# Modulation tiles issued earlier and attention's steps reordered in a two-layer hybrid transformer kernel

## The chip, the cores and the metric

One core of one Trainium2 chip runs the whole kernel. The metric is the device time of one execution in microseconds, as the median of several runs. Of the engines, PE is TensorE (PEld its weight load), DVE is VectorE, ACT is ScalarE, POOL is GpSimd, and SP (SyncE) issues DMAs.

## The reference, cut to what matters

Two layers over 256 latent tokens and 256 context tokens, width 1024. Each layer is a half-step SwiGLU, a token mixer and a half-step SwiGLU, and each of the three is scaled, shifted and gated by a modulation vector of nine parts:

```python
mod_l = (jax.nn.silu(c) @ w_mod[i] + b_mod[i]).reshape(b, N_MOD, 1, D_MODEL)
mod_c = (jax.nn.silu(c_ctx) @ w_mod[i] + b_mod[i]).reshape(N_MOD, 1, D_MODEL)
x_lat = x_lat + 0.5 * mod_l[:, 2] * swiglu(modulate(x_lat, norm_gain[i, 0], mod_l[:, 0], mod_l[:, 1]), ffn_a_in[i], ffn_a_out[i])
...
def neighbourhood_attention(q, k, v, k_ctx, v_ctx, rpb):
    s = jnp.concatenate([s_win.reshape(b, h, GRID_W, n_win), s_ctx], axis=-1)
    p = jax.nn.softmax(s, axis=-1).astype(v.dtype)
def dense_attention(q, k, v):
    p = jax.nn.softmax(s, axis=-1).astype(v.dtype)
```

The mixer of layer 0 is attention (8 heads) beside a long convolution, that of layer 1 is retention with 4 heads. Both streams, latent and context, pass through it; only the latents come out of the last layer.

## The kernel before, in words

Every matrix product is made of three TensorE products, high by high, low by high, high by low, so each weight tile (128x1024) is split into a high and a low part: ACT copies the high part (`whi`, line 92), DVE subtracts it for the low part (`wlo`, line 186). A call of `w_get` splits three tiles ahead of the one it hands out. The order on each engine is the order of the calls in the program; nothing is reordered. PSUM tiles of the pool `ps` have seven buffers.

The modulation vectors of all but the first two parts are 128 tiles of `w_mod` (128x1024 each), read in a fixed order (layer 0 parts 2 to 8, then layer 1). `mod_step` takes the next one: DVE multiplies the tile by the conditioning row and sums it up (`junk`, line 272), twice, once per stream, or once for parts 5 to 8 of layer 1 (tile 96 onwards); then `m_dma` issues the load of the next tile from POOL's queue (line 257). The two buffers of `wm` mean that this load waits for the reduction of the tile before. Where `mod_step` is called is written out by hand at each place.

The stages in order, with their place in the trace: the first SwiGLU of layer 0 (`ffn`, about 57 to 413 us, 22 pairs of input tiles in three pieces, each piece followed by `out_gemm`); the attention and convolution mixer (`mixer0`, to 668); two SwiGLUs in which most products are made of seven instead of eight half products (`ffn_fast` with class `Fast`, to 1375; its first piece makes pairs 2 and 3 in the plain way, then starts the seven-product pairs with `ramp` and `cycle`); retention (`mixer1`, to 1667); the last SwiGLU on the latents alone (`ffn` with `lat_only`).

In `mixer0` the loop `for i in range(12)` makes one projected tile per step and calls `attend(i)`. For head pair b = i // 2, an even step makes the latents' scores (`scores_lat`), an odd one the context's (`scores_ctx`); each returns a closure for the exponentials (`exps`, ACT) and one for the normalisation (`norm`, DVE). The even step after that transposes both heads' probabilities (`transposes`: per head two latent blocks `ptp`, one context block `ptc`), and the odd one after it multiplies them by the values. The scores' high and low parts of queries and keys come from `qk_split`. `z_conv` makes the short convolution's tile of each step between them.

In `mixer1` each of the 4 heads does `qk_parts` (POOL makes the low parts, line 974), four `tiles` of the values' projection with `mod_step` between them, the split of the values (`vlo`, line 216) which frees the four PSUM buffers `pv`, two `tiles` of the gate, and the next head's `scores` (`pst`).

Of the kernel before, what the change touches and what calls it, by code (L numbers as in the profile page):

```python
# [57 lines left out]
def body(ctx, tc, I, out):  # L58
# [550 lines left out]
    def in_tile(n0=0, n1=TOK, ahead=3):  # L609
        return tile_mm(w_get(ahead), n0, n1)  # L610
# [243 lines left out]
    def ffn_fast(i, l, n, norm_in, norm_out):  # L854
        fast = None
        for h, (jf, jl) in enumerate(PIECES):
            Gt = []
            last = h == len(PIECES) - 1

            def evac(pa, pb):  # L860
                sg = page(name="sg")
                act(sg, pa, AF.Silu)
                V.tensor_tensor(out=sg, in0=sg, in1=pb, op=ALU.mult)
                g = (page(dt=F32R, name="ghi"), page(dt=F32R, name="glo"))
                split_to(sg, g[0], g[1])
                drop(sg)
                Gt.append(g)

            if h == 0:
                p = first_group(norm_in, lambda p: evac(p[0], p[1]))  # L870
                hs = half_sums(norm_in)
                evac(p[2], p[3])
                next(hs)
                for j in range(2, FAST[i]):
                    end = j == FAST[i] - 1
                    wa, wb = w_get(), w_get()
                    pa = tile_mm(wa)
                    next(hs, None)
                    if end:
                        fast = Fast(jl - FAST[i])  # L880
                        fast.ramp()
                    else:
                        w_split()
                    pb = tile_mm(wb)
                    next(hs, None)
                    evac(pa, pb)
                    if not end:
                        mod_step()
                next(hs, None)
            Gt.extend(fast.run())  # L890
            if last:
                h_free()
            if h == 0:
                set_gate(l, n)
            pend_free.extend(Gt)

            def ramp():
                nonlocal fast
                fast = Fast(PIECES[h + 1][1] - PIECES[h + 1][0])
                fast.ramp()  # L900

            out_gemm(Gt, jl - jf, 1, l, n, False, norm_out if last else None,
                     ramp=None if last else ramp, mods=2 if last else KB - 1)
            free_acts()

    def ffn(l, n, norm_in, norm_out, lat_only=False):
        w = L if lat_only else TOK
        for h, (jf, jl) in enumerate(PIECES):
            Gt = []
            last = h == len(PIECES) - 1  # L910

            def evac(pa, pb, shift=None):
                sg = page([P, w], name="sg")
                if shift is None:
                    act(sg, pa[:, :w], AF.Silu)
                    V.tensor_tensor(out=sg, in0=sg, in1=pb[:, :w], op=ALU.mult)  # L916
                else:
                    act(sg, pa[:, :w], AF.Silu, bias=shift[:, 0:1])
                    V.scalar_tensor_tensor(out=sg, in0=pb[:, :w], scalar=shift[:, 1:2], in1=sg,
                                           op0=ALU.add, op1=ALU.mult)  # L920
                g = (page([P, w], F32R, "ghi"), page([P, w], F32R, "glo"))
                split_to(sg, g[0], g[1])
                drop(sg)
                Gt.append(g)

            j0 = 0
            if h == 0:
                if norm_in is None:
                    q, cs = pre.pop("first")
                    w_split()  # L930
                    for t in range(0, 6, 2):
                        if t:
                            w_split()
                        evac(q[t], q[t + 1], cs[:, t:t + 2])
                    w_split()
                    drop(*q)
                elif callable(norm_in):
                    p = norm_in()
                    evac(p[0], p[1])
                    evac(p[2], p[3])  # L940
                else:
                    p = first_group(norm_in, lambda p: evac(p[0], p[1]))
                    evac(p[2], p[3])
                j0 = len(Gt)
            for j in range(jf + j0, jl):
                pa = in_tile(0, w)
                pb = in_tile(0, w)
                evac(pa, pb)
                full = next(FILT["gen"], True)
                if not lat_only or j < 5:  # L950
                    mod_step(1 if lat_only or not full else 2)
            if last:
                h_free()
            if h == 0:
                set_gate(l, n)
            pend_free.extend(Gt)
            out_gemm(Gt, jl - jf, 1, l, n, lat_only, norm_out if last else None, mods=2 if last else KB)
            free_acts()
# [296 lines left out]
    def mixer0(norm_in, norm_out):  # L1255
# [145 lines left out]
            return prc, exps, norm  # L1401

        def transposes(prs, prc):
            pt = [page([P, 2, 256], name="pt") for _ in range(2)]
            for qb in range(2):
                p = ps([P, 4, P], name="ptp")
                for kb in range(4):
                    T.transpose(p[:, kb, :], prs[qb][:, kb * P:(kb + 1) * P], ident)
                for i in range(2):
                    dst = pt[i][:, :, qb * P:(qb + 1) * P]  # L1410
                    if i:
                        V.tensor_copy(dst, p[:, 2 * i:2 * i + 2, :])
                    else:
                        act(dst, p[:, 2 * i:2 * i + 2, :], AF.Copy)
            p = ps([P, 2, 2, P], name="ptc")
            for qb in range(2):
                for kb in range(2):
                    T.transpose(p[:, kb, qb, :], prc[:, qb, kb * P:(kb + 1) * P], ident)
            ptc = page([P, 2, 256], name="ptc")
            act(ptc, p.rearrange("p a b c -> p a (b c)"), AF.Copy)  # L1420
            drop(*prs, prc)
            return pt, ptc

        def values(b, turned):

# [16 lines left out]
        def attend(i):  # L1442

            b, odd = divmod(i, 2)
            if odd and b - 1 in turned:
                values(b - 1, turned.pop(b - 1))
            if not odd and b - 1 in lat:
                prs, prc = lat.pop(b - 1)[0], con.pop(b - 1)[0]
                turned[b - 1] = [transposes(prs[j], prc[j]) for j in range(2)]
            if b < 4 and not odd:  # L1450
                lat[b] = scores_lat(b)
                left.append(lat[b][1:])
            if b < 4 and odd:
                con[b] = scores_ctx(b)
                left.append(con[b][1:])
                for a in qks.pop(b):
                    drop(*a)
                for j in range(2):
                    load_bias(2 * b + 2 + j)


        blkr = one.tile([P, P], F32R, name="blkr")
# [20 lines left out]
        for c in range(2):  # L1483
            w = [w_get(), w_get(2)]
            for tb in range(4):
# [7 lines left out]
                    T.matmul(o, lhsT=H[k][1][:, hs_], rhs=wk[0][:, ws_], start=False, stop=k == KB - 1)  # L1493
                if (c, tb) in ((0, 1), (1, 0)):
                    qk_step()
            mod_step(2)
        for tb in range(4):
            vt.append(page(name="vt"))
            act(vt[tb], pv[tb], AF.Copy)

        qk_split(0)
        load_bias(0)
        load_bias(1)
        dft = []
# [25 lines left out]
        for i in range(12):  # L1530
            p = in_tile()
            attend(i)
            if i < 8:
                ex, nor = left.pop(0)
                c = z_conv(i // 2, p, i % 2 == 0)
                if i % 2 == 0:
                    next(c)
                    ex()
                    next(c, None)
                    held = nor  # L1540
                else:
                    held()
                    ex()
                    next(c)
                    nor()
                    if i < 7:
                        qk_split(i // 2 + 1)
                    next(c, None)
            else:
                x0c.extend(conv(p, i - 8, "x0c"))  # L1550
            if i in (2, 4, 6, 8):
# [60 lines left out]
    def mixer1(norm_in, norm_out):  # L1612
# [33 lines left out]
        for h in range(4):  # L1646
            pa, pb = in_tile(0, L), in_tile(0, L)
            q = page(name="qT")
            rope_to(q[:, :L], q[:, L:], pa[:, :L], pb[:, :L])
            qT.append(q)  # L1650
            if h % 2:
                mod_step()
            if h == 0:
                parted(kT[0], 0)
                parted(kT[0], 1)
            if h == 1:
                parted(qT, 0)
# [106 lines left out]
        for h in range(4):  # L1764
# [2 lines left out]
            pv = [ps(name="pv") for _ in range(4)]  # L1767
            for n in range(4):
                tiles(4, pv, n)
                if n in (1, 2):  # L1770
                    mod_step(2)
                if n == 0 and prev:
                    o_trans(h - 1, prev)
            vh = []
            for tb in range(4):
                vh.append((page(dt=F32R, name="vhi"), page(dt=F32R, name="vlo")))
# [164 lines left out]
```

## Time and profile before

| | |
|---|---|
| median of 3 runs | 1862.87 us (1859.59, 1862.87, 1862.88) |
| profiled execution, its own time | 1861.55 us |
| its span, first to last instruction | 1859.8 us |
| PE busy | 1823.5 us, 98% |
| DVE busy | 1403.1 us, 75% |
| ACT busy | 828.8 us, 45% |
| POOL busy | 195.7 us, 11% |
| DMA | 306 MB, 165 GB/s |
| reductions of modulation tiles (line 272) | 224, 289.1 us of DVE |

Busy times say how long an engine had an instruction in work. In the timeline each row has the start in us from the span's start, the duration of the merged run of instructions, the engine, the line, the operation, what it writes and reads, the shapes, their number, and in brackets how long the engine stood idle before it and what ended that.

### The profile page before, as it was taken

The page shows a single profiled execution, that of the slowest core. Times are in us where ns is not written, and L with a number is a line of the kernel's source. Part 1 is how long each engine was busy: PE and PEld are TensorE (multiplying, and loading weights), DVE is VectorE, ACT ScalarE, POOL GpSimd, SP SyncE. Part 2 cuts the span into 40 slices and gives each one's busy share as a digit, 9 for nine tenths or more (in the row PEclk, how much of TensorE's full clock was granted, in tenths as well). Part 3 has the DMA queues.
Part 4 walks back from the last instruction along what each step waited for, and adds up shares of the span by engine and source line. Part 5 has one row for each costly group of instructions (what it writes and reads, how often), then busy time and mean ns, then how long its engine had stood idle before and what let it go on. Part 6 is the DMA issues. An engine that isn't in the chain of part 4 may idle for free.

```text
span 1859.8 us, 28832 instructions
## 1 busy us (share of the span) xinstructions
PE 1823.5 (98%) x11264; PEld 1606.0 (86%) x11264; DVE 1403.1 (75%) x2303; ACT 828.8 (45%) x1388; POOL 195.7 (11%) x271
## 2 busy tenths in 40 slices
PE   7999999999999999999999999999999899999999
PEld 4788888888777898898998889989999788899999
DVE  6678797777877878888876788778777776687554
ACT  4422222245564356264464653626543354455443
POOL 2020010001102100111110001111001111000000
PEclk9999999999999999999999999999999999999999
DMA  9446565532422334576673356757635444475563
GB/s 358 174 165 216 171 214 184 189 125 80 159 69 91 125 108 125 171 193 195 174 215 114 80 174 180 209 164 198 200 103 175 137 140 155 159 242 171 179 200 105
DMA packets 98074, 306.01 MB, mean 165 GB/s; under 512 B 10897, under 2 KB 11921, under 8 KB 97810
## 3 DMA queue, kind: packets, MB, share of 16 engines
q1 hardware_dynamic: 67986, 216.08, 34.7%
q0 software_dynamic: 29952, 88.09, 17.9%
q8 instruction: 88, 1.44, 0.3%
q14 instruction: 48, 0.39, 0.1%
HBM read 303.08 MB, written 1.05 MB: 164 GB/s over the span
## 4 chain that ended last, share of the span: by engine, by line
PE 56%; DVE 7%; issue 5%; ACT 4%; DMA 1%; POOL 0%; POOLq 0%; ACTq 0%; DVEq 0%
PE pA L709 9%; PE po L245 6%; PE po L244 6%; PE po L243 6%; PE pC L709 5%; PE pi L243 3%; PE pi L245 3%; PE pi L244 3%; PE pB L709 2%; PE fg L244 1%; PE fg L243 1%; PE fg L245 1%; PE pv L1685 1%; PE pv L1683 1%; PE pv L1684 1%
## 5 line engine op out<-in xcount | busy, mean ns | idle before, releaser
L92 ACT ACTIVATE whi<-raw 128x1024 fp32r<-128x1024 f32 (+2 forms) x434 | 422.1, 1000 | 267.6 <-PE po L244 119.3
L186 DVE TENSOR_TENSOR wlo<-raw,whi 128x1024 fp32r<-128x1024 f32 (+1 forms) x286 | 340.8, 1212 | 65.5 <-ACT whi L92 64.0
L243 PE MATMUL pi<-hhi,whi 128*128 128x512 f32 (+1 forms) x912 | 318.8, 350 | 0.2 <-ACT ptc L92 0.2
L245 PE MATMUL pi<-hhi,wlo 128*128 128x512 f32 (+1 forms) x912 | 318.1, 349 | 0.0
L244 PE MATMUL pi<-hlo,whi 128*128 128x512 f32 (+1 forms) x912 | 317.4, 348 | 0.0
L272 DVE CUSTOM_DVE_ANT_0 junk<-wm,scb,cst 128x1024 bf16<-128x1024 f32 x224 | 289.1, 1291 | 30.7 <-DMA wm<-in_wmt_dram 26.4
L243 PE MATMUL po<-ghi,whi 128*128 128x512 f32 (+1 forms) x776 | 269.9, 348 | 0.3 <-ACT ghi L92 0.3
L244 PE MATMUL po<-glo,whi 128*128 128x512 f32 (+1 forms) x776 | 269.5, 347 | 0.1
L245 PE MATMUL po<-ghi,wlo 128*128 128x512 f32 (+1 forms) x776 | 269.6, 347 | 0.0
L243 PEld LDWEIGHTS pi<-hhi,whi 128*128 128x128 f32 x912 | 171.7, 188 | 26.8 <-issue 1.5
L245 PEld LDWEIGHTS pi<-hhi,wlo 128*128 128x128 f32 x912 | 171.5, 188 | 23.7
L244 PEld LDWEIGHTS pi<-hlo,whi 128*128 128x128 f32 x912 | 171.6, 188 | 23.6
L695 DVE TENSOR_TENSOR wlo<-raw,whi 128x1024 fp32r<-128x1024 f32 (+1 forms) x144 | 153.7, 1088 | 43.9 <-ACT whi L92 43.4
L243 PEld LDWEIGHTS po<-ghi,whi 128*128 128x128 f32 x776 | 145.9, 188 | 20.4 <-ACT ghi L92 0.5
L244 PEld LDWEIGHTS po<-glo,whi 128*128 128x128 f32 x776 | 145.9, 188 | 20.4 <-DVE glo L216 0.3
L245 PEld LDWEIGHTS po<-ghi,wlo 128*128 128x128 f32 x776 | 145.9, 188 | 19.9
L257 POOL DMA_DIRECT2D wm<-in_wmt_dram x128 | 71.2, 556 | 857.3 <-DVE mod L272 838.2
L434 DVE SCALAR_TENSOR_TENSOR x<-po,gate,x 128x256 f32<-128x256 f32 x192 | 86.4, 479 | 59.8 <-PE po L245 59.4
L92 ACT ACTIVATE ghi<-sg 128x512 fp32r<-128x512 f32 (+1 forms) x52 | 28.2, 541 | 183.3 <-DVE sg L916 172.3
L709 PE MATMUL pC<-hlo,whi 128*128 128x256 f32 x288 | 81.0, 281 | 0.6 <-DVE hlo L216 0.6
L709 PE MATMUL pC<-hhi,wlo 128*128 128x256 f32 x288 | 81.1, 282 | 0.1
L709 PE MATMUL pC<-hhi,whi 128*128 128x256 f32 x288 | 80.5, 279 | 0.0
(405 smaller groups left out, 3897.6 us busy)
## 6 DMA issues: line engine op xcount, KB each, us to landing
raw<-in_ffi_dram SPq DMA_DIRECT2D x176, 512.0 KB, 4.4
wm<-in_wmt_dram POOLq DMA_DIRECT2D x128, 512.0 KB, 3.9
raw<-in_rt_dram SPq DMA_DIRECT2D x64, 512.0 KB, 4.3
raw<-in_ffo_dram SPq DMA_DIRECT2D x64, 448.0 KB, 4.1
raw<-in_ffi_dram POOLq DMA_DIRECT2D x72, 256.0 KB, 5.7
raw<-in_ffo_dram SPq DMA_DIRECT2D x32, 512.0 KB, 4.5
raw<-in_ev_dram SPq DMA_DIRECT2D x32, 512.0 KB, 4.3
raw<-in_ffi_dram SPq DMA_DIRECT2D x36, 256.0 KB, 3.7
```

The costliest lines, as they stand in the source:

```text
L92: S.activation(out=out, in_=in_, func=func, **k)
L186: V.tensor_tensor(out=lo[:, :n], in0=t[:, :n], in1=f(hi[:, :n]), op=ALU.subtract)
L243: T.matmul(o, lhsT=w[0][:, c0:c1], rhs=x[0][:, x0:x1], start=start, stop=False)
L244: T.matmul(o, lhsT=w[0][:, c0:c1], rhs=x[1][:, x0:x1], start=False, stop=False)
L245: T.matmul(o, lhsT=w[1][:, c0:c1], rhs=x[0][:, x0:x1], start=False, stop=stop)
L257: G.dma_start(out=t, in_=I["wmt"][n])
L272: V.tensor_tensor_reduce(out=junk, in0=t, in1=scb[:, s, :], scale=1.0, scalar=bcol, op0=ALU.mult, op1=ALU.add, accum_out=MOD[l][:, idx, b, ...
L434: V.scalar_tensor_tensor(out=xs(s, m), in0=p[:, c0:c0 + L], scalar=gate[:, m, s:s + 1], in1=xs(s, m), op0=ALU.mult, op1=ALU.add)
L695: V.tensor_tensor(out=w[1][:, :c], in0=src, in1=f(w[0][:, :c]), op=ALU.subtract)
L709: T.matmul(o, lhsT=w[a][:, c0 + j * P:c0 + (j + 1) * P], rhs=x(j)[b][:, x0(j):x0(j) + L], start=first and j + a + b == 0, stop=j == 3 and ...
L1683: T.matmul(po[tb], lhsT=H[k][0][:, hs_], rhs=w[0][:, ws_], start=k == 0, stop=False)
L1684: T.matmul(po[tb], lhsT=H[k][0][:, hs_], rhs=w[1][:, ws_], start=False, stop=False)
```

## The change

In `ffn_fast` the `mod_step` after the last plain pair is dropped. In `ffn` of layer 0 seven pairs (j = 8, 10, 12, 15, 17, 18, 20) get one more, between their two products; the last `ffn` gets one more, at j = 5. In `mixer0` the second `mod_step(2)` of the values' projection becomes one `mod_step` after `qk_split(0)`. In `mixer1` the one at h = 3 of the query projections goes, and the four per head (two after each of tiles 1 and 2) become three (one after each of tiles 0, 1 and 2). The number of tiles in all stays 128.

In attention the latents' normalisation follows its exponentials in the same step instead of standing over to the next one; `qk_split(b + 1)` moves ahead of the exponentials of the odd step; the context's normalisation comes after the convolution's tile is done; and the transposes take both heads' four latent blocks first and then the two context blocks.

```diff
@@ ffn_fast
                     evac(pa, pb)
-                    if not end:
-                        mod_step()
@@ ffn
                 pa = in_tile(0, w)
+                if not lat_only and j in (8, 10, 12, 15, 17, 18, 20):
+                    mod_step()
                 pb = in_tile(0, w)
                 evac(pa, pb)
                 full = next(FILT["gen"], True)
-                if not lat_only or j < 5:
+                if not lat_only or j < 6:
                     mod_step(1 if lat_only or not full else 2)
@@ transposes (prs, prc are now of both heads)
+            pt = [[page([P, 2, 256], name="pt") for _ in range(2)] for _ in range(2)]
+            for j in range(2):
+                for qb in range(2):
+                    p = ps([P, 4, P], name="ptp")
...
+                drop(*prs[j])
+            ptc = []
+            for j in range(2):
+                p = ps([P, 2, 2, P], name="ptc")
...
+                ptc.append(page([P, 2, 256], name="ptc"))
+                act(ptc[j], p.rearrange("p a b c -> p a (b c)"), AF.Copy)
+                drop(prc[j])
+            return list(zip(pt, ptc))
@@ attend
-                turned[b - 1] = [transposes(prs[j], prc[j]) for j in range(2)]
+                turned[b - 1] = transposes(prs, prc)
...
                     load_bias(2 * b + 2 + j)
+                if b < 3:
+                    qk_split(b + 1)
@@ values' projection of mixer0
-            mod_step(2)
+            if c == 0:
+                mod_step(2)
...
         qk_split(0)
+        mod_step()
@@ loop over i of mixer0
-                if i % 2 == 0:
-                    next(c)
-                    ex()
-                    next(c, None)
-                    held = nor
-                else:
-                    held()
-                    ex()
-                    next(c)
-                    nor()
-                    if i < 7:
-                        qk_split(i // 2 + 1)
-                    next(c, None)
+                next(c)
+                ex()
+                next(c, None)
+                nor()
@@ mixer1, query projections and heads
-            if h % 2:
+            if h == 1:
                 mod_step()
...
-                if n in (1, 2):
-                    mod_step(2)
                 if n == 0 and prev:
                     o_trans(h - 1, prev)
+                if n < 3:
+                    mod_step()
```

## Rows read from the trace of the kernel before

**Rows 1.** The page's first part: busy time, share and instructions of each engine.
```profile
PE 1823.5 (98%) x11264; PEld 1606.0 (86%) x11264; DVE 1403.1 (75%) x2303; ACT 828.8 (45%) x1388; POOL 195.7 (11%) x271
```
**Rows 2.** PE's waits by releaser: total us, times, longest us.
```profile
PE pst L243 <- DVE vlo L216: 7.4, 1, 7.4
...
PE psc L1342 <- DVE qklo L216: 0.8, 1, 0.8
...
PE ptp L1408 <- DVE pr L1373: 0.8, 2, 0.6
```
**Rows 3.** Stretches: start:end length, busy us of each engine, granted clock, DMA share, GB/s.
```profile
125.00:400.00 275.00, 275.00 (x1201) 223.21 (x1200) 224.34 (x335) 75.16 (x97) 25.87 (x49) 1.00 0.57 192
...
513.40:516.70 3.30, 3.30 (x14) 2.12 (x11) 3.23 (x10) 0.23 (x1) 0.00 (x0) 0.50 0.00 0
...
1471.20:1478.60 7.40, 0.13 (x2) 0.00 (x0) 5.46 (x10) 0.00 (x0) 1.05 (x2) 0.81 0.58 213
1478.60:1482.60 4.00, 3.90 (x15) 3.71 (x16) 3.57 (x6) 0.39 (x1) 0.00 (x0) 0.50 0.44 135
...
714.00:727.00 13.00, 10.04 (x73) 8.73 (x72) 11.30 (x17) 7.95 (x16) 0.00 (x0) 1.00 0.15 44
```
**Rows 4.** Timeline of DVE, ACT and PE at the first start of seven-product pairs.
```profile
709.26 1.28 DVE L272 CUSTOM_DVE_ANT_0 junk<-wm,scb,cst 128x1024 bf16<-128x1024 f32 x1
...
712.13 0.42 DVE L631 TENSOR_TENSOR sx<-hf 128x256 f32<-128x256 f32 x1
...
708.52 1.69 ACT L92 ACTIVATE hf<-hf,mod 128x256 f32<-128x256 f32 x4
...
722.47 0.38 PE L709 MATMUL pA<-syhi,whi 128*128 128x256 f32 x1 [0.98 <-ACT qa L92]
```
**Rows 5.** Timeline of DVE and POOL in retention's first head.
```profile
1445.63 1.28 DVE L272 CUSTOM_DVE_ANT_0 junk<-wm,scb,cst 128x1024 bf16<-128x1024 f32 x1
...
1470.04 1.28 DVE L272 CUSTOM_DVE_ANT_0 junk<-wm,scb,cst 128x1024 bf16<-128x1024 f32 x1 [5.08 <-DMA wm<-in_wmt_dram]
...
1475.61 1.28 DVE L272 CUSTOM_DVE_ANT_0 junk<-wm,scb,cst 128x1024 bf16<-128x1024 f32 x1 [1.94 <-DMA wm<-in_wmt_dram]
...
1477.96 2.48 DVE L216 TENSOR_TENSOR vlo<-pv,vhi 128x512 fp32r<-128x512 f32 x4
...
1459.14 1.29 POOL L974 TENSOR_TENSOR flo<-kb,fhi 128x512 fp32r<-128x512 f32 x1
1460.40 2.28 POOL L974 TENSOR_TENSOR flo<-qT,fhi 128x512 fp32r<-128x512 f32 x1
1462.62 0.57 POOL L257 DMA_DIRECT2D wm<-in_wmt_dram  x1
```
**Rows 6.** Timeline of DVE and PE in attention's first round.
```profile
485.85 1.28 DVE L272 CUSTOM_DVE_ANT_0 junk<-wm,scb,cst 128x1024 bf16<-128x1024 f32 x1
...
503.27 1.23 DVE L186 TENSOR_TENSOR wlo<-raw,whi 128x1024 fp32r<-128x1024 f32 x1 [3.47 <-ACT whi L92]
...
508.17 1.14 DVE L1398 TENSOR_SCALAR prc<-prc,sm 128x256 f32<-128x256 f32 x4
509.23 1.29 DVE L216 TENSOR_TENSOR qklo<-qy,qkhi 128x512 fp32r<-128x512 f32 x2
...
511.99 0.69 DVE L1298 TENSOR_TENSOR x1c<-x1c,vc 128x512 f32<-128x512 f32 x1
...
511.67 0.66 PE L1418 MATMUL ptc<-cst,prc 128*128 128x128 f32 x4 [1.49 <-ACT ptc L92]
```
**Rows 7.** Timeline of DVE and PE where the last SwiGLU's first piece ends.
```profile
1707.69 2.10 DVE L186 TENSOR_TENSOR wlo<-raw,whi 128x896 fp32r<-128x896 f32 x2 [0.42 <-ACT whi L92]
...
1710.62 0.38 PE L243 MATMUL po<-ghi,whi 128*128 128x256 f32 x1 [0.29 <-ACT ghi L92]
```
**Rows 8.** DVE's wait for PE in layer 0's first SwiGLU; the tiles' loads, issue to landing.
```profile
206.83 0.69 DVE L916 TENSOR_TENSOR sg<-sg,pi 128x512 f32<-128x512 f32 x1 [1.63 <-PE pi L245]
...
DMA to landing us min/median/max: 3.6/4.0/10.5
```

More of the change, by code (lines that the diff above doesn't have):

```diff
@@ L1403, in transposes @@
         def transposes(prs, prc):
[L1404 to L1412, printed above, removed]
-                    else:
[L1414 to L1422, printed above, removed]
+            pt = [[page([P, 2, 256], name="pt") for _ in range(2)] for _ in range(2)]
+            for j in range(2):
+                for qb in range(2):
+                    p = ps([P, 4, P], name="ptp")
+                    for kb in range(4):
+                        T.transpose(p[:, kb, :], prs[j][qb][:, kb * P:(kb + 1) * P], ident)
+                    for i in range(2):
+                        dst = pt[j][i][:, :, qb * P:(qb + 1) * P]
+                        if i:
+                            V.tensor_copy(dst, p[:, 2 * i:2 * i + 2, :])
+                        else:
+                            act(dst, p[:, 2 * i:2 * i + 2, :], AF.Copy)
+                drop(*prs[j])
+            ptc = []
+            for j in range(2):
+                p = ps([P, 2, 2, P], name="ptc")
+                for qb in range(2):
+                    for kb in range(2):
+                        T.transpose(p[:, kb, qb, :], prc[j][:, qb, kb * P:(kb + 1) * P], ident)
+                ptc.append(page([P, 2, 256], name="ptc"))
+                act(ptc[j], p.rearrange("p a b c -> p a (b c)"), AF.Copy)
+                drop(prc[j])
+            return list(zip(pt, ptc))
         def values(b, turned):
@@ L1535, in mixer0 @@
                 c = z_conv(i // 2, p, i % 2 == 0)
-                if i % 2 == 0:
-                    next(c)
-                    ex()
-                    next(c, None)
-                    held = nor
-                else:
-                    held()
-                    ex()
-                    next(c)
-                    nor()
-                    if i < 7:
-                        qk_split(i // 2 + 1)
-                    next(c, None)
+                next(c)
+                ex()
+                next(c, None)
+                nor()
             else:
```

## The prediction

> **What bounds the kernel now.** I read the busy times first: PE has work in 98% of the span, no other engine over 75% [rows 1]. A product always in work is not a product at full rate, so the next view is PE's waits. They are few, and one is by far the longest: 7.4 us in retention's first head, for DVE's split of the values [rows 2]. The view by stretches then says where DVE is the one that is late: in most of the kernel PE is busy without a break (125 to 400 us: 275.00 of 275) while DVE has 50.7 us to spare; at the start of the seven-product pairs PE loses 13.00 - 10.04 = 2.96 us, and the same pattern comes a second time at 1067; in attention and in the first head there are stretches where the granted clock reads 0.50, the lower of its two levels (1.2 for 2.4 GHz), after PE had stood or nearly stood [rows 3]. So an instruction of DVE costs time only where it stands ahead of one of these waits, and a reduction is free elsewhere. The timelines of those places are rows 4 to 7. The number of reductions doesn't change; only their places do.
>
> **The two starts of seven-product pairs.** The dropped step is two reductions of 1.28 on DVE, back to back, from 709.26. The first operation behind them that needs all four of ACT's copies (`hf`, ending at 708.52 + 1.69 = 710.21) is line 631, which began at 712.13 [rows 4]. Without the reductions it begins at 710.25: 1.87 us earlier. Everything up to PE's wait for ACT's copy `qa` hangs on it in one chain that passes between DVE and ACT. PE itself must still do its products between the waits: moving every release by 1.87 takes away the first waits and leaves about 1.1 of 2.96. Gain 1.9 a start, **3.7** for both. Ends: 3.0, if one of ACT's own operations is late next, and 2 x 2.56 = 5.1, all of the reductions' time. The step's load goes from POOL's queue, where loads of the seven-product weights stood behind it; that can only help.
>
> **Attention.** The four reductions from 485.85 stood ahead of the first low parts `qklo`, for which PE waited 0.8 [rows 2, 6]. Now the low parts come first and two reductions after them: 0.8 gained, and DVE reaches the first scores some 1.4 us earlier. In the first round DVE idled 3.47 us until ACT's exponentials and a weight's high part were done [rows 6]; the normalisation of the latents now fills about 1 us of that, and PE's 0.8 for `pr` [rows 2] goes. The context's normalisation, done at 508.17 + 1.14 = 509.3, gets `qklo` (1.29), two convolution steps (0.75 each) and the product (0.69) ahead of it [rows 6], 3.5 in all, less 1.4 and 1.0: it ends at about 510.2. PE comes to the context's transposes at about 507 and waits some 2.6 us there. That is as much as the waits it had among the transposes, but it comes after the latents' blocks and not between: the 1.49 for a context block's copy [rows 6] is mostly gone, and the next scores begin about 0.7 sooner, beyond the 0.8. The stretch at half clock behind it (3.30 us at 0.50 [rows 3], worth 1.65) I leave standing, as the sum of the waits is about the same. Rounds two to four: the latents' blocks are copied four transposes earlier, so the scores no longer wait for the buffers; PE's waits there were a few tenths each, and I take 1.2 for all. **2.7** in sum; ends -1 (the context's normalisation late in each round) and 5.5 (the clock doesn't fall, and no wait is left).
>
> **Retention's first head.** Two steps go ahead of the split of the values: the reduction at 1445.63 in the projections and the fourth of the head [rows 5]. DVE was busy without a break behind the first, and ACT and POOL (the splits of `qk_parts`, line 974) followed from it, so all of it moves 1.2 us up, the load issued at 1462.62 too. The second reduction still waits for that load, which is behind POOL's three splits as before; I take its landing as 1.2 earlier. The third tile's load now waits for nothing, and the fourth reduction with its own wait goes: 1.28 + 1.94 [rows 5] = 3.2. The split of the values then begins at 1477.96 - 4.4 = 1473.6. PE stands 3.0 us, not 7.4. Behind the 7.4 the clock was at 0.50 for 4.0 us [rows 3], which is 2.0 lost; after 3.0 us I take it not to fall, since PE lost 2.96 in 13 us at 714 with the clock at 1.00 throughout [rows 3]. Gain 4.4 + 2.0 = **6.4**. Ends: 3.2 (landing no earlier, clock falls all the same) and 9.4 (no wait at all). In the later heads PE had no such wait and DVE waited for PE; the reduction at tile 0 now stands ahead of the weights' splits there, behind cover, at no cost.
>
> Here a rule bears. POOL's third split took 2.28 where the one before took 1.29 [rows 5]; DVE was splitting weights meanwhile. The Trainium skill (SBUF — State Buffer, section "SBUF: two separate sides") says that a DVE operation with two SBUF inputs and a GpSimd operation that reads SBUF take shared ports as an exclusive lock, the second one blocked until the first ends. By that rule the reduction moved to tile 0, which has two SBUF inputs, delays POOL and the load by its length, and the sum of the whole change is 10.7 and not 12.0; the stretched split agrees with it. It is one of the rivals.
>
> **The last SwiGLU.** One more reduction at j = 5: DVE had 0.42 idle there, so what follows is 1.28 - 0.42 = 0.86 later, and PE waits at 1710.62 for the last pair's parts already (0.29) [rows 7]. Cost **0.8**; ends 0.5 and 1.3.
>
> **Layer 0's first SwiGLU.** Seven steps of 2 x 1.28, 18 us, into 50.7 us of idle DVE [rows 3]. The tightest pair shown leaves 1.63 us in which DVE waits for PE [rows 8]: a pair with the extra step runs 1 us late and the next makes it up (17 and 18 together 2). What hides it: weights are split three tiles ahead, 3 x 24 products of 275/1201 = 0.23 [rows 3], 16.5 us. Cost 0; if the cover were gone, 18 us. The loads add 3.7 MB to a stage at 192 GB/s [rows 3], 13 GB/s more, and land in 4.0 us in the middle [rows 8]; the weights' loads are on SP's queue and pass no step.
>
> **Sum.** 3.7 + 2.7 + 6.4 - 0.8 = 12.0, from the profiled execution's 1861.55: **1849.5**. That execution lies 1.3 under the median of the runs and between the lowest and the highest. What a measurement of this kernel can tell from no change is about 0.2%, 3.7 us.
>
> **Rivals.**
> Attention gives nothing: `prc` is late in every round, since DVE now stands still for the exponentials in the even steps. For: the latents' normalisation holds up the weight's split behind it. Against: DVE idled in that place anyway (3.47). Worth 2.7 less: 1852.2. Chance 0.15; at its end of -1, 1853.2.
> The first head's load lands as late as before, or the clock falls behind the shorter wait: 1.2 to 3.2 less, up to 1852.7. For: four transfers share that stretch (DMA share 0.58 at 1471 [rows 3], landings up to 10.5 [rows 8]). Chance 0.15.
> POOL's last split is stretched by the moved reduction: 1.28 less, 1850.8. For: 2.28 against 1.29 [rows 5]. Against: the weights' split that it replaces in that place did the same. Chance 0.1.
> Slower: in layer 0's first SwiGLU the extra steps wait for their loads. With the longest landing of 10.5 [rows 8] each takes 13.1 of DVE, seven 92, against 50.7 idle and 16.5 of cover: PE stands 25 us, 1874. It turns the sign from (50.7 + 16.5 + 12.0) / 7 - 2.6 = 8.7 us of wait a step on. Against: between two steps half a pair's products lie, and the median landing is 4.0. Chance 0.04.
> The change does not do what it says: the PSUM and SBUF buffers that the new order is given make other waits as long as those removed, in attention and the first head both: within 0.2%, 1858 to 1865. Chance 0.08; slower than that 0.01.
>
> **Numbers.** The forecast itself 0.47, the three partial cases 0.40, together faster 0.87; same 0.08; slower 0.05. Range: all upper ends, 5.1 + 5.5 + 9.4 - 0.5 = 19.5, give 1842; all lower ends, 3.0 - 1 + 3.2 - 1.3 = 3.9, give 1857.6. The corners are unlikely, so 1843 to 1857 leaves out the two last rivals and little more.
>
> **What would show it.** PE's wait for `vlo` at about 3 us and no clock of 0.50 behind it; under 1.3 us lost in each of the two starts, with no wait for a weight's high part; no wait for `qklo`, one wait of 2 to 3 us for `prc` in the first round; a wait of about 1.1 us for `ghi` at the last SwiGLU's first piece; PE busy 275 of 275 in layer 0's first SwiGLU. It is wrong if PE waits there, if `prc` is waited for in every round, or if the wait for `vlo` stays over 5 us.

## The result, and the profile after

The changed kernel took 1847.88 us in the median (1845.95 to 1850.75), 0.9921 of the kernel before, with a 95% interval of 0.9907 to 0.9935. Forecast were 1849.5 and a range of 1843 to 1857. The profiled execution has a span of 1845.4 us against 1859.8, 14.4 less; twelve were forecast. The page's first part, which answers to [rows 1], says that DVE's work is the same (224 reductions still) and PE's share one point higher:

```profile
PE 1819.8 (99%) x11264; PEld 1605.3 (87%) x11264; DVE 1402.8 (76%) x2303; ACT 830.0 (45%) x1388; POOL 196.2 (11%) x271
```

PE's waits by releaser (total us, times, longest us) answer to [rows 2]. The wait for `vlo` is too short to be listed (0.13 us), and those for `qklo` and `pr` are gone. The wait for `prc` has grown from 0.4 to 2.2 us and the one for `ghi` from 0.3 to 0.8; both are in the kernel before, though not among the lines of [rows 2]:

```profile
PE pA L709 <- ACT qa L92: 3.2, 3, 1.2
PE ptc L1423 <- DVE prc L1398: 2.2, 1, 2.2
...
PE po L243 <- ACT ghi L92: 0.8, 1, 0.8
...
PE pC L709 <- DVE hlo L216: 0.6, 2, 0.3
PE pA L709 <- DVE wlo L695: 0.6, 2, 0.3
PE psc L1342 <- ACT ptc L92: 0.5, 2, 0.3
```

The view by stretches (length, busy us of PE, PEld, DVE, ACT and POOL, granted clock, DMA share, GB/s) answers to [rows 3]: layer 0's first SwiGLU, the first start of seven-product pairs (7.3 us earlier now), the stretch behind attention's first round, and the first head's.

```profile
125.00:400.00 275.00, 275.00 (x1202) 223.30 (x1201) 241.67 (x363) 74.95 (x97) 29.68 (x56) 1.00 0.61 205
...
510.40:513.81 3.41, 3.35 (x12) 2.11 (x12) 3.34 (x10) 1.18 (x3) 0.00 (x0) 0.50 0.01 2
...
1463.40:1466.40 3.00, 2.87 (x21) 2.49 (x20) 3.00 (x5) 0.00 (x0) 0.00 (x0) 1.00 0.88 321
706.70:719.70 13.00, 11.43 (x81) 10.33 (x80) 11.29 (x17) 8.00 (x16) 0.00 (x0) 1.00 0.16 42
```

Layer 0's first SwiGLU took 17.3 us more of DVE and PE lost nothing. A start costs PE 1.57 us of idle time and not 2.96. In the first head there is no stretch at half clock any more, in attention there still is.

Where the 14.4 went can be read by taking the start of one and the same product in both traces. Two such products, in PE's timeline of the changed kernel, stood at 722.47 [rows 4] and 1710.62 [rows 7] before, so the gain is 7.3 us behind the first start and 15.0 at the end of the last SwiGLU's first piece:

```profile
715.21 0.39 PE L709 MATMUL pA<-syhi,whi 128*128 128x256 f32 x1 [0.97 <-ACT qa L92]
...
1695.66 0.38 PE L243 MATMUL po<-ghi,whi 128*128 128x256 f32 x1 [0.77 <-ACT ghi L92]
```

Read in this way from place to place, the changed kernel gains 5.4 us between program start and the end of attention, 1.9 at each of the two starts, and 8.4 in the first head. It loses 1.3 behind the second start, 0.5 at the end of the last SwiGLU's first piece, and 1.4 spread over stretches in which PE waits for nothing. The timeline of DVE and POOL in the first head answers to [rows 5]:

```profile
1450.94 1.75 DVE L186 TENSOR_TENSOR wlo<-raw,whi 128x1024 fp32r<-128x1024 f32 x1 [1.82 <-ACT whi L92]
1452.62 2.32 DVE L272 CUSTOM_DVE_ANT_0 junk<-wm,scb,cst 128x1024 bf16<-128x1024 f32 x1
...
1458.47 1.28 DVE L272 CUSTOM_DVE_ANT_0 junk<-wm,scb,cst 128x1024 bf16<-128x1024 f32 x1 [2.38 <-DMA wm<-in_wmt_dram]
...
1460.82 1.28 DVE L272 CUSTOM_DVE_ANT_0 junk<-wm,scb,cst 128x1024 bf16<-128x1024 f32 x1
...
1463.16 2.47 DVE L216 TENSOR_TENSOR vlo<-pv,vhi 128x512 fp32r<-128x512 f32 x4
```

```profile
1451.56 2.30 POOL L974 TENSOR_TENSOR flo<-qT,fhi 128x512 fp32r<-128x512 f32 x1
1453.80 0.58 POOL L257 DMA_DIRECT2D wm<-in_wmt_dram  x1
```

The second reduction began 4.7 us after POOL issued its load; before the change it was 7.4 (1462.62 to 1470.04 [rows 5]). No term of the forecast held this shorter landing.

### The profile page after: what moved, and what is told of

It is laid out like the page before. It is cut to its first block, busy times and chain, and to the rows that moved or that the text cites. A ratio compares the mean times of both kernels' runs of the same rounds, so it can differ in the third digit from the quotient of the medians.

```text
span 1845.4 us, 28831 instructions
## 1 busy us (share of the span) xinstructions
PE 1819.8 (99%) x11264; PEld 1605.3 (87%) x11264; DVE 1402.8 (76%) x2303; ACT 830.0 (45%) x1388; POOL 196.2 (11%) x271
## 4 chain that ended last, share of the span: by engine, by line
PE 60%; DVE 6%; ACT 3%; issue 3%; DMA 1%; POOL 0%; ACTq 0%; DVEq 0%; POOLq 0%
PE pA L709 10%; PE po L244 7%; PE po L245 7%; PE po L243 7%; PE pC L709 5%; PE pi L243 3%; PE pi L245 3%; PE pi L244 3%; PE pB L709 2%; PE fg L245 1%; PE fg L243 1%; PE fg L244 1%; PE pv L1685 1%; PE pv L1684 1%; PE pv L1683 1%
```

## The experiments

Each kernel's ratio to the kernel before carries about 0.0015 either way; the changed kernel's is 0.9920 in the mean of two sets of runs, and 0.001 is 1.9 us. The difference between two kernels then carries some 3 to 3.6 us. Of the differences below, 7.6, 7 and 5 are clear of that, 3.7 barely is, and 3.2, 3 and 2.4 are not: for these the traces, of one execution each, have to decide.

**The two starts undone** (two of layer 0's steps go for them):

```diff
                     evac(pa, pb)
+                    if not end:
+                        mod_step()
-                if not lat_only and j in (8, 10, 12, 15, 17, 18, 20):
+                if not lat_only and j in (8, 10, 12, 15, 17):
```

> The changed kernel with the two dropped steps of ffn_fast put back (two of layer 0's extra steps, j = 18 and 20, go for them). Theory, each place pays for itself by DVE's order: each start loses 1.9 us again, but in the second the half load that DVE waited 1.67 us for in the changed kernel (PE 1.23 us, at 1087) is in time again, so the whole is 1.9 + 1.9 - 1.3 = 2.5 us slower than the changed kernel, about 1850.4 against 1847.9. Rival, that half load is late because of the kernel as a whole and not of the earlier start: PE still waits 1.2 us there, and the whole is 3.7 slower, 1851.6.

0.9940 (0.9928 to 0.9952), median 1851.62: 3.7 slower, the rival's number. The waits of the starts are back as before, and the one 20 us behind the second start is there too: `qa` 4 times with up to 1.1, in PE's waits from 700 to 1100 us:

```profile
PE pA L709 <- ACT qa L92: 3.4, 4, 1.1
PE pA L709 <- DVE wlo L695: 2.1, 4, 0.8
PE pA L709 <- ACT whi L92: 1.2, 2, 0.6
```

So the 1.3 that the changed kernel's profile lost behind the second start comes without the earlier start too (1.1 here). Over the profiled kernels with the change's starts that wait was between nothing and 1.3.

**Retention's steps undone** (five of layer 0's go):

```diff
-            if h == 1:
+            if h % 2:
                 mod_step()
...
+                if n in (1, 2):
+                    mod_step(2)
                 if n == 0 and prev:
                     o_trans(h - 1, prev)
-                if n < 3:
-                    mod_step()
```

> The changed kernel with retention's steps as before (h = 1 and 3, two tiles after each of tiles 1 and 2 of a head; five of layer 0's extra steps go). Theory: PE stands some 7 us for vlo in the first head again, with the clock at half speed for some 4 us behind it; 8.5 us slower than the changed kernel, 1856.4. Rival, the changed kernel owes a part to a load that happened to land early (4.5 us after its issue, against 7.4 before), which has to do with what other loads are under way and not with the steps: PE then stands 4.5 us and loses 5 to 6 in all, 1853.4.

0.9961 (0.9948 to 0.9974), median 1855.12: 7.6 slower, nearer to the theory. But the profiled execution, the fastest of its six (1851.68), shows the rival's trace: a wait of 4.5 us, and the clock at half for 3.41 us behind it.

```profile
PE pst L243 <- DVE vlo L216: 4.5, 1, 4.5
```

```profile
1467.00:1470.41 3.41, 3.09 (x13) 3.06 (x14) 3.41 (x6) 0.00 (x0) 0.00 (x0) 0.50 0.49 154
```

The same steps in this head stand 7.4 us in one execution (the kernel before) and 4.5 in another. Both statements hold: the steps cost 7.6 in the middle, and single executions scatter by the loads' landing: the load behind POOL's splits landed in 7.3 us there and in 4.4 here.

**Only the fourth step in each head put back** (four of layer 0's go):

```diff
                 if n < 3:
-                    mod_step()
+                    mod_step(1 + n // 2)
```

> The changed kernel with four tiles in each head (one, one, two; four of layer 0's extra steps go). Theory, by the prediction's own term: the fourth reduction of the first head waits for its load, issued when the second reduction ends; it comes 1.9 to 2.7 us later than the third's end and the split of the values with it, so PE stands 2.5 to 4.5 us for vlo, and the clock is at half for 3.4 us behind it in most executions: 2.7 to 5 us slower than the changed kernel, 1851.5. Rival, the fourth step is hidden as the third one is, and the gain came from the earlier first step alone: within 1 us of the changed kernel.

0.9937 (0.9921 to 0.9954), median 1851.56: 3.2 slower. The profiled execution was the slowest of four and stood 6.3 us, with the clock at half for 6.8 us from 1469.3 on.

```profile
PE pst L243 <- DVE vlo L216: 6.3, 1, 6.3
```

Its DVE timeline shows why: each reduction behind the first waits for its own load, and the third's came 8 us after its issue at 1457.75.

```profile
1460.79 1.28 DVE L272 CUSTOM_DVE_ANT_0 junk<-wm,scb,cst 128x1024 bf16<-128x1024 f32 x1 [2.19 <-DMA wm<-in_wmt_dram]
...
1465.81 1.28 DVE L272 CUSTOM_DVE_ANT_0 junk<-wm,scb,cst 128x1024 bf16<-128x1024 f32 x1 [2.60 <-DMA wm<-in_wmt_dram]
...
1469.44 1.29 DVE L272 CUSTOM_DVE_ANT_0 junk<-wm,scb,cst 128x1024 bf16<-128x1024 f32 x1 [2.34 <-DMA wm<-in_wmt_dram]
```

The fourth reduction's wait for a load of its own (2.34 us) is shown, and with it the kind of cost that the prediction took for this step (1.28 + 1.94 = 3.2). That the median's 3.2 is the same number shows little: it carries 3.6 either way, and this execution lost far more.

**Attention's order undone, the tiles left** (`transposes`, `attend` and the loop of `mixer0` as in the lines that the diff of the change removes).

> The changed kernel with attention's order as before, the tiles where the change put them. Theory: the scores of two heads run as pairs of instructions at the same time in the changed kernel, and a wait for a buffer in the old order takes the pairs apart; so rounds two to four lose some 3.0 us and the first some 1.4, 4.4 in all, 1852.3. Rival, the working of the prediction: the waits themselves are all that is lost, some 0.4 a round; with the first round 1.9 to 2.6 in all, 1850.1.

0.9933 (0.9920 to 0.9945), median 1849.23: 2.4 slower, in the rival's range, but with 3 us either way the times don't tell the two apart. The trace agrees with the theory on the mechanism. From the end of the first round to the end of attention this kernel loses 3.3 us on the changed one. The timeline of PE in the second round's scores, of this kernel and then of the changed one, has one row per merged run of products:

```profile
531.99 0.49 PE L1342 MATMUL psc<-qkhi 64*128 64x512 f32 x1
532.75 0.49 PE L1342 MATMUL psc<-qkhi 64*128 64x512 f32 x1 [0.26 <-ACT ptc L92]
532.75 0.72 PE L1342 MATMUL psc<-qklo,qkhi 64*128 64x512 f32 x2
533.09 0.61 PE L1342 MATMUL psc<-qkhi,qklo 64*128 64x512 f32 x2
533.95 0.83 PE L1342 MATMUL psc<-qkhi 64*128 64x512 f32 x2 [0.25 <-DVE pt L1412]
534.29 0.71 PE L1342 MATMUL psc<-qklo,qkhi 64*128 64x512 f32 x2
534.63 0.61 PE L1342 MATMUL psc<-qkhi,qklo 64*128 64x512 f32 x2
```

```profile
532.42 0.50 PE L1342 MATMUL psc<-qkhi 64*128 64x512 f32 x2 [0.30 <-ACT ptc L92]
532.75 0.40 PE L1342 MATMUL psc<-qklo,qkhi 64*128 64x512 f32 x2
532.99 0.39 PE L1342 MATMUL psc<-qkhi,qklo 64*128 64x512 f32 x2
533.22 0.40 PE L1342 MATMUL psc<-qkhi 64*128 64x512 f32 x2
533.45 0.39 PE L1342 MATMUL psc<-qklo,qkhi 64*128 64x512 f32 x2
533.68 0.39 PE L1342 MATMUL psc<-qkhi,qklo 64*128 64x512 f32 x2
```

Two products of 64 rows, one for each head, run at the same time: two of them take 0.50 together. If the first of a pair gets its buffer and the second has to wait, the pairs come apart: twelve products take 3.2 us and not 1.6, with only 0.5 us of waits among them. In the third round they take 3.2 too, and 2.0 in the changed kernel.

That the times show 2.4 and not 3.3 or more is within what they carry. The clock behind the first round doesn't explain it. In the changed kernel it falls behind the wait of 2.2 us in five of the seven profiled executions that have that wait (for 3.4 us, or 6.8); where it did not fall, in the second execution of the changed kernel, that was worth 1.3 us. In this kernel's one profiled execution it stayed at 1.00 behind several short waits, but behind the same short waits it fell in the kernel before [rows 3]. Over whole executions the mean granted clock is 0.998 in both kernels (five executions of this one, nine of the changed one).

**Only the transposes' order undone** (per head two latent blocks, then the context block):

```diff
-                turned[b - 1] = transposes(prs, prc)
+                turned[b - 1] = [transposes(prs[j], prc[j]) for j in range(2)]
```

> The changed kernel with only the transposes' order as before (per head two latent blocks, then the context block). Theory, it is this order that makes the scores of rounds two to four wait for buffers and takes their pairs apart: PE loses some 1.0 us a round again, 3 in all, and the first round's wait for prc comes earlier by four transposes with the four latent ones behind it: 3 to 3.5 slower than the changed kernel by the trace. Rival, the early normalisation and the early low parts do it, and the transposes' order gives nothing: 0.5 or less, pairs unbroken.

0.9903 (0.9889 to 0.9917), median 1844.67: not slower but 3 faster, at the edge of what the times tell. The theory falls: the pairs stay whole in rounds two to four (1.7 and 1.9 us for twelve products), PE's only wait in all of attention is the first round's (3.2 us, and in the profiled execution 6.83 us at half clock behind it).

```profile
PE ptc L1418 <- DVE prc L1398: 3.2, 1, 3.2
```

So it isn't the latents' blocks first that keeps the pairs whole; that part of the change gave nothing here. What is left of the change to attention is the early normalisation and the early low parts, and the run with the low parts later, below, leaves the early normalisation. The profiled execution of this kernel was the slowest of its five and has a span 0.7 us over the changed kernel's profiled one; in it some 1.7 us are gained by PE's pace in later stages without any wait, which is what the run with the pages turned is about.

**The last SwiGLU's extra step undone** (a step at j = 14 of layer 0 for it):

> The changed kernel with the step at j = 5 of the last SwiGLU moved to layer 0's first SwiGLU (j = 14). Theory: PE's wait for ghi at the end of the first piece falls from 0.77 to 0.29 us and nothing is late in layer 0: 0.5 to 1.0 us faster, 1847.1. Rival, layer 0's first SwiGLU is full with seven steps and the eighth is waited for: 1 to 2.5 us slower.

0.9925 (0.9912 to 0.9938), median 1847.61: no difference that can be told. In the trace PE doesn't wait in that place at all, 0.77 less, and layer 0 hides the eighth step. Its first head is the other thing to see: the change's own steps, and yet a wait of 1.9 us for `vlo` and the clock at half behind it.

```profile
PE pst L243 <- DVE vlo L216: 1.9, 1, 1.9
```

**The changed kernel once more.**

> The changed kernel once more, for its spread. Two theories of what is the same and what is not between two executions: the waits that DVE's order sets (2.2 us for prc, 1.2 us at each start's qa) are the same to 0.1 us, while the stretches at half clock (3.4 or 6.8 us long, behind attention's first round, in the inverse transform, in retention's first head) and the landing of the second and third tile's loads in that head (4.4 to 7.2 us) come and go; the runs then spread over some 5 us, 1846 to 1851. Rival: the spread comes from the start of the program (the first constants' load), and the rest is fixed; then the spans differ by less than 0.5 us behind 30 us.

0.9919 (0.9905 to 0.9933), 1845.65 to 1850.04. The theory holds: the wait for `prc` is 2.2 again, that for `ghi` 0.8, while `vlo` has 1.3 (0.13 in the first profile) and the clock doesn't fall in attention:

```profile
PE ptc L1423 <- DVE prc L1398: 2.2, 1, 2.2
...
PE pst L243 <- DVE vlo L216: 1.3, 1, 1.3
```

**More tiles to layer 0** (four fewer in the late places; the expectation's "five" is a slip):

```diff
-                if not lat_only and j in (8, 10, 12, 15, 17, 18, 20):
+                if not lat_only and j in (5, 6, 8, 10, 12, 13, 14, 15, 17, 18, 20):
...
-                if not lat_only or j < 6:
+                if not lat_only or j < 5:
...
         qk_split(0)
-        mod_step()
...
-                if n < 3:
+                if n < (3 if h else 1):
                     mod_step()
```

> The changed kernel with five more tiles taken from where DVE is late: the step behind the first low parts of attention, the one at j = 5 of the last SwiGLU, the second and third step of retention's first head; four of them go to layer 0's first SwiGLU (11 steps, j = 5, 6, 8, 10, 12, 13, 14, 15, 17, 18, 20). Theory: the wait for prc falls from 2.2 to about 0.9 us, that for ghi from 0.8 to 0.3, that for vlo to nothing in every execution; layer 0 pays nothing: 2.5 to 4 us faster than the changed kernel. Rival: layer 0's steps now wait for their loads and DVE for the tiles, and PE stands in layer 0: 1 to 10 us slower.

0.9947 (0.9934 to 0.9961), median 1852.97: 5 slower. The other places did roughly as expected (`prc` 1.5 where 0.9 was expected, `ghi` of the last SwiGLU 0.3, no wait for `vlo`), but at the end of layer 0's first piece PE stood 4.7 us, with the clock at half from near the end of that wait on:

```profile
PE po L243 <- ACT ghi L92: 4.7, 1, 4.7
```

```profile
128.00:134.80 6.80, 5.41 (x12) 4.00 (x13) 6.00 (x10) 3.63 (x5) 0.53 (x1) 0.50 0.54 174
```

In that piece POOL makes four splits (97.5 to 104.5 us) ahead of the tiles' loads, and DVE waits 6.3 us for one of them:

```profile
DVE junk L272 <- DMA wm<-in_wmt_dram: 6.8, 2, 6.3
```

The changed kernel has that wait too (6.45 us) and loses nothing by it. Two steps more behind it, at j = 5 and 6, are four reductions of 1.28 and 0.5 us more of waiting for loads; DVE's last product of the piece comes 5.6 us later, and that comes out in the last pair's `ghi`. This is near the prediction's rival for the slower side and not the same: there the extra steps' own loads were to be late, here it is the steps' own work behind a load that is late in any case, in the piece that the change leaves alone.

**The same without the first piece, and the transposes' old order**: j = 7, 8, 9, 10, 12, 13, 14, 15, 17, 18, 20, the rest as above.

> The changed kernel with the transposes' order as before, and four tiles fewer where DVE is late (the step behind the first low parts, the one at j = 5 of the last SwiGLU, the second and third step of retention's first head), four more in layer 0's first SwiGLU but none in its first piece (j = 7, 8, 9, 10, 12, 13, 14, 15, 17, 18, 20). Theory: layer 0 hides eleven steps as long as they keep out of the first piece; the transposes' order gives 3, the steps 0.7 for ghi, 1.3 for prc and 1 to 3 for vlo and the clock behind it: 1841.5, six faster than the changed kernel. Rival: eleven steps are too many anywhere, PE stands for ghi at a piece's end in layer 0 by 2 us and more, and the kernel is no faster than with the transposes' order alone, 1844.7 or slower.

0.9881 (0.9866 to 0.9896), median 1842.04: some 7 faster than the changed kernel. PE waits 0.5 us for `ghi` once in layer 0, and the first head has neither a wait nor a fall:

```profile
1461.00:1470.00 9.00, 9.00 (x44) 7.43 (x43) 6.30 (x10) 4.97 (x7) 0.00 (x0) 1.00 0.10 39
```

**The next round's low parts later**, in that kernel:

```diff
-                if b < 3:
-                    qk_split(b + 1)
...
                 nor()
+                if i % 2 and i < 7:
+                    qk_split(i // 2 + 1)
```

> The kernel of the run before it, with the next round's low parts of queries and keys split behind the context's normalisation, as in the kernel before, and not ahead of the exponentials. Theory, what is ahead of prc on DVE sets PE's wait in the first round: prc comes 1.3 us earlier, its wait falls below 1 us, and the clock doesn't fall behind it: 1 to 2 us faster than the run before. Rival: the low parts are late for the scores in rounds two to four (0.3 to 1 us each, pairs taken apart), and it is as fast or up to 2 us slower.

0.9893 (0.9876 to 0.9910), median 1843.78: not told apart from the run before it. The wait for `prc` falls from 2.5 to 1.2 (under 1 was expected), but PE now waits 0.9 for the context blocks' copies at the first round's scores, which takes the gain back, and the last stage runs 1.1 us slower with no wait in it.

```profile
PE ptc L1418 <- DVE prc L1398: 1.2, 1, 1.2
...
PE psc L1342 <- ACT ptc L92: 0.9, 2, 0.5
```

In rounds two and three the twelve products still take 1.9 and 1.8 us. So the low parts need not be early for the pairs to stay whole, and the early normalisation is what is left; it was not undone alone.

**Pages turned.** Tiles lie in SBUF pages that are taken from the front of a list and put back at its end.

```diff
     mixer0(nm[0, 1], nm[0, 2])
+    for _ in range(3):
+        drop(page())
```

> The changed kernel with the list of free SBUF pages turned by three places between the mixer and the SwiGLU behind it; no instruction is added, removed or moved. Theory: the pace of PE's products in stretches without a wait hangs on which pages the operands lie in (the last 145 us took 143.98 before, 144.56 in the changed kernel and 143.44 with the transposes' order undone, with the same instructions). Then that stretch takes another time than 144.56, by 0.2 to 1.5 us, while everything up to the mixer's end stays. Rival: the pace comes from where the instructions lie or from what ran before; then the last stretch takes 144.56 again, to 0.05.

0.9908 (0.9893 to 0.9922), median 1846.86. In the last stage the 240 products `pi` of line 245 (duration min/median/max, first and last start) stand in the changed kernel, in its second execution, with the pages turned, with the transposes undone, and in the kernel before:

```profile
L245 PE MATMUL pi<-hhi,wlo x240: 277/283/287, 1714.1 to 1819.0; 128*128 128x256 f32 x120
```

```profile
L245 PE MATMUL pi<-hhi,wlo x240: 278/283/287, 1714.5 to 1819.5; 128*128 128x256 f32 x120
```

```profile
L245 PE MATMUL pi<-hhi,wlo x240: 276/280/286, 1713.6 to 1817.9; 128*128 128x256 f32 x120
```

```profile
L245 PE MATMUL pi<-hhi,wlo x240: 274/278/287, 1716.0 to 1819.6; 128*128 128x256 f32 x120
```

```profile
L245 PE MATMUL pi<-hhi,wlo x240: 276/281/286, 1729.0 to 1833.4; 128*128 128x256 f32 x120
```

The stretch takes 104.9, 104.9, 104.3, 103.7 and 104.4 us with the same instructions and no wait. It goes with the kernel and not with the execution or the chip: it is 104.9 in five profiled executions with the change's order of attention, on different chips, and 103.7 again, on another chip, in the run with eleven steps, which has the transposes' old order too. The whole last stage takes 144.56 us in the changed kernel and 143.92 with the pages turned. So one half of the theory holds: with no instruction added or moved the pace changes, by some 0.6 us in 145. The other half doesn't: everything up to the mixer's end should have stayed, but the products `pi` of line 245 in layer 0's first SwiGLU, ahead of the place where the list is turned, take 310.5 us with the pages turned, and 310.1 in both executions of the changed kernel:

```profile
L245 PE MATMUL pi<-hhi,wlo x320: 388/394/403, 57.6 to 368.1; 128*128 128x512 f32 x160
```

That the place of the operands sets the pace is thus not shown. What is shown is that the pace differs from program to program, by up to 1.2 us in this stretch, and not from execution to execution.

## Why the prediction was right, point by point

**The starts, 3.7**: right, by the time of the kernel that undoes them (3.7) and by the products' starts (1.9 each). What was left of PE's idle time was 1.57 and not 1.1, so the sign "under 1.3" did not come. The gain came out all the same, since two waits of five, 1.4 us, are gone at each start, and a wait costs PE some 0.27 us beyond its idle time: the product ahead of it counts 0.28 as busy where products in a row start 0.12 apart, and behind the waiting product the next one begins after 0.22 and not 0.12. The 1.3 lost behind the second start in the profile is a half load's landing, which comes and goes.

**The first head, 6.4**: 8.4 in the profiled pair, 7.6 by the kernel that undoes it. The step that was mis-sized is "I take its landing as 1.2 earlier". The landing itself took 4.5 us and not 7.3, so the split of the values began at 1463.16; in the time of the kernel before (7.6 later there) that is 1470.8, not 1473.6, and PE stood 0.13 us and not 3.0. The 7.3 was one execution's: in the twelve other profiled executions the load behind POOL's splits landed in 4.3 to 5.3 us, with the old steps (4.4) as with the new. Why it was late in that one is not shown. In other executions the change's steps give waits of up to 1.9 us, as the two loads land later. The step "after 3.0 us I take it not to fall" isn't safe either: the clock fell behind 1.9 us in one execution, and not behind 1.6 in the one with the starts undone.

**Attention, 2.7**: 5.4 in the profiled pair up to its end; by the kernel that undoes the order 2.4 (3 either way), beside what the moved tile gave at `qklo` (1.0 in the trace, 0.8 forecast). The first round went as worked out, with one wait for `prc` (2.2 us where 2.6 were forecast) and the half clock behind it; up to its end the gain was 2.4 where the 0.8 and 0.7 were taken. (The terms given for the end of the normalisation add up to 510.4 and not 510.2; it ended at 509.8.) The term that was too small is "I take 1.2 for all" of rounds two to four: they gave 2.9, since waits among the scores cost the pairs and not only their own length. Its reason was wrong as well: "the latents' blocks are copied four transposes earlier" is not what frees the scores, for with the old order of the transposes the pairs stay whole too.

**The last SwiGLU, -0.8**: -0.5 in the trace (the wait for `ghi` is 0.77 where it was 0.29 and 1.1 was forecast), too little for the times. **Layer 0, nothing**: right where the steps were put, and 5 us in the kernel that put two into the first piece.

**The rivals.** The slower one did not come; the first of the runs with eleven steps shows a place where extra steps do make PE late, by another way. The rule on shared ports (the Trainium skill, SBUF — State Buffer, section "SBUF: two separate sides") was weighed as a delay of POOL. The Trainium skill says there that whichever of the two instructions starts first has the ports for the whole of it. The trace agrees, and each side loses in turn. POOL's second split stands ahead of the rows shown above:

```profile
1450.31 1.31 POOL L974 TENSOR_TENSOR flo<-kb,fhi 128x512 fp32r<-128x512 f32 x1
```

DVE's weights' split, POOL's third split and the reduction then overlap, take 1.75, 2.30 and 2.32 us, and each ends 1.07, 1.17 and 1.08 us behind the end of the one ahead of it on the other engine, somewhat less than its length alone (1.23 [rows 6], 1.31, 1.28). So POOL's third split is held up by the weights' split, as before the change (2.28 [rows 5]), and it is the reduction that waits for POOL and not the other way round. Before the change two weights' splits stood there and took 4.00, in DVE's timeline of the kernel before:

```profile
1459.76 4.00 DVE L186 TENSOR_TENSOR wlo<-raw,whi 128x1024 fp32r<-128x1024 f32 x2 [1.82 <-ACT whi L92]
```

So the moved reduction, in the place of the second of these, cost the load nothing, and the 1.28 of that rival are refuted.

**The sum** was 12.0, against 14.4 between the profiled spans and 15.0 between the medians. The three undone parts cost 3.7 + 7.6 + 2.4 = 13.7, each with some 3 us either way; with the 1.0 at `qklo` less the 0.5 of the last SwiGLU, both from the trace, that is 14.2. All terms were right in place and sign, but part of the closeness is luck. In the profiled pair the first head gave 2.0 and attention 2.7 more than forecast; the late half load took 1.3 of that back and the pace 1.4, and neither was in the forecast.

## What to carry to other kernels

A PE that is 98% busy can still be sped up by moving work between places of another engine: look for the few waits that DVE ends, and move what stands ahead of them to a stage where DVE waits for PE, away from any point at which a queue of loads is held up. A step that waits for a load of its own costs its wait at a place where DVE is late, and that wait scatters from execution to execution; in the three kernels that take the second and third load out of the first head that wait is gone. Undo each part alone before trusting it: here one part of the change gave nothing, and its opposite with four more moved tiles was 7 us faster.

## What the runs showed of the hardware that was not expected

- Two products of 64 rows in different halves of the rows run at the same time (0.50 us for both, starts 0.003 apart). Two waits of 0.26 and 0.25 among twelve such products cost 1.6 us in all. The Trainium skill (TensorE: Matmul & The Clock Gate, section "Part 3: Packing small matmuls — row/col tiling") says that products in different rows of the array run concurrently with starts some 4 ns apart, and the trace agrees; what waits between them cost was new.
- PE's pace without a wait differs from program to program and repeats from execution to execution: 103.7 to 104.9 us for the same products. What sets it is not shown.
- The stretches at half clock were 3.4 or 6.8 us long wherever they were looked at, and came and went between executions, behind the same wait of 2.2 us. In three of the seven executions with that wait the clock fell once more, for 3.4 us, at about 616 us, and cost 1.5 us there.
- The second load in the first head, issued at the same point of the program with the same loads around it, took from 4.9 to 7.9 us to land.
